# Second projection of a squared-ReLU MLP: weight loads in GpSimd's queue, residual rows summed a tile ahead, output finished in place, two early weight slots

## The chip, the core and the metric

The kernel runs on one core of one Trainium2 chip. The metric is the device time in microseconds of one execution, and what is compared is the median of several. The names of the engines are those of the profile: PE is TensorE, DVE VectorE, ACT ScalarE, POOL GpSimd, and SP SyncE, which here only issues DMA transfers.

## What is computed

One layer over 2048 rows of 1024 float32 numbers: a mixer of four head groups with its projections, then an MLP of inner width 4096 with a squared ReLU. The change concerns only the product with `w_ff2` and the sum behind it:

```python
x = x + (y @ w_out[l]).astype(x.dtype)
h = rmsnorm(x, norm_ffn[l])
x = x + (jnp.square(jax.nn.relu(h @ w_ff1[l])) @ w_ff2[l]).astype(x.dtype)
```

## The kernel before

A float32 product is made of three passes over operands that are split into a high and a low part (high by high, high by low, low by high; `PASS`). Both MLP products use one level of Strassen's method: the operands are cut into quarters, and seven products of sums of quarters replace eight. The second projection thus has seven products, in the order n = 0 to 6 (`AT` gives their numbers). Each has eight row tiles q of 128 rows by 512 columns, here written (n,q), and each tile is 16 units of the inner dimension by three passes, 48 matmuls of 128x128 by 128x512, into one PSUM bank. There are two banks, so tile (n,q+2) needs the bank of tile (n,q).

**Weights.** A unit is 128x512 of a sum of quarters of `w_ff2`. `t_unit` loads raw quarters with `raw512` into a ring of six buffers (`wr`): one for n = 0, 1, 2, three for n = 3, two for n = 4, 5, 6. DVE forms the sums by `tsub` (L1217; two for n = 3, one for n = 4, 5, 6). For n = 3 the sum is also stored to DRAM (`tt`, L1506, from GpSimd's queue), from where n = 5 loads it. `split` makes the high part on ACT (`wh`, L1207) and the low part on DVE (`wl`, L1208). The 26 slots for split units are used in turn: 9 in the ring pool (`wh`/`wl`), 15 in a pool `t2p` (`vh`/`vl`, also named wh and wl in the profile), one in buffers named `xr`, and one in `gain` (`wg`). `t2p` lies where the first projection kept its operands, so what is written there first waits until these have been stored to DRAM (`as`). Ten units of product n + 1 find a slot free while product n runs; the last six can be split only when units of n are used for the last time, in its tile q = 7. `t_unit` calls are spread over the tiles q = 3 to 7 and run at raised priority.

**Rows.** `s_tile` loads the 128 rows of a tile (the squared ReLU's Strassen operand, which the first projection stored in `as`) in two halves `sr` of 512 KB, and splits them on ACT (L1519) and DVE (L1520) into `st`, of which there are two, one tile ahead.

**Results.** A PSUM bank is emptied by ACT (n = 0, into `X`) or by sums on DVE: with `X` or into `Y`, or into the output. `finish` gives the output for n = 1, 5 and 6 (two for each tile there): it loads the residual rows `x1` into a buffer `tq` (of eight), adds `X` or `Y` to them, adds PSUM to that into a second `tq`, and stores this.

All loads and stores but those to `tt` are issued by SP, in one order for all, and a transfer that waits for its buffer holds up those behind it. A scheduler fixes the order of each engine's instructions at build time, by priority and an estimate of times; on the chip each engine goes through its list in order.

Of the kernel before, what the change touches and what calls it, by code (L numbers as in the profile page):

```python
# [16 lines left out]
ALU = mybir.AluOpType  # L17
# [4 lines left out]
P = 128  # L22
T = 2048
D = 1024
TB = 512
# [6 lines left out]
NW = 9  # L32
# [27 lines left out]
def emit(ctx, tc, a):  # L60
    nc = tc.nc
    V, S, G, PE, SY = nc.vector, nc.scalar, nc.gpsimd, nc.tensor, nc.sync
# [5 lines left out]
    x1_d = [dram.tile([TB, D], F32, name=f"x1d{b}") for b in range(NB)]  # L68
# [48 lines left out]
    c1 = p1.enter_context(tc.tile_pool(name="c1", bufs=1))  # L117
# [7 lines left out]
    def psum_mm():  # L125
        return mm.tile([P, 512], F32, tag="mm", name="mm")
# [40 lines left out]
    for r in range(2):  # L167
        G.dma_start(out=sink[r * 64:(r + 1) * 64, :],
                     in_=a["attn_sinks"].rearrange("(k r) -> r k", r=2)[r].partition_broadcast(64),
# [1028 lines left out]
    tt_d = dram.tile([NJ, P, 512], F32, name="tt")  # L1198
# [5 lines left out]
    def split(raw, pool=ring, tags=("wh", "wl"), bufs=NW):  # L1204
        h = pool.tile([P, 512], F32R, tag=tags[0], name="wh", bufs=bufs)
        l = pool.tile([P, 512], F32R, tag=tags[1], name="wl", bufs=bufs)
        S.activation(out=h, in_=raw, func=AF.Copy)  # L1207
        V.tensor_tensor(out=l, in0=raw, in1=h, op=ALU.subtract)  # L1208
        return h, l

    def raw512(src):
        r = ring.tile([P, 512], F32, tag="wr", name="wr", bufs=NR)
        SY.dma_start(out=r.rearrange("p (k c) -> p k c", k=4) if len(src.shape) == 3 else r, in_=src)
        return r

    def tsub(o, x, y, op=ALU.subtract):
        V.tensor_tensor(out=o, in0=x, in1=y, op=op)  # L1217
# [112 lines left out]
    def w2(k, half, nd):  # L1330
        return a["w_ff2"][(2 * k + half) * P:(2 * k + half + 1) * P, nd * 512:(nd + 1) * 512]


    def w_units(j, tmp, tw=None):
        f0 = j * 2 * P

        def raw(kh, fh):
            return raw512(a["w_ff1"][kh * 512:(kh + 1) * 512, f0 + fh * P:f0 + (fh + 1) * P]
                          .rearrange("(k p) c -> p k c", p=P))

        with hi_():
            a11, a12, a21, a22 = raw(0, 0), raw(1, 0), raw(0, 1), raw(1, 1)
            u = [split(a11), split(a12)]
            s1, s2 = (tw or tmpw)(), (tw or tmpw)()
            tsub(s1, a21, a22, ALU.add)
            tsub(s2, s1, a11)
            u.append(split(s2))
            u.append(split(s1))
            s3, s4 = tmp(), tmp()
            tsub(s3, a11, a21)  # L1350
            u.append(split(s3))
            tsub(s4, a12, s2)
            u.append(split(s4))
            u.append(split(a22))
        return u
# [116 lines left out]
    def tmp2():  # L1472
        return t2p.tile([P, 512], F32, tag="tq", name="tq", bufs=NT2)

    units = [0]
    NB2 = 15

    def split2(raw):
        n = units[0] % (NW + NB2 + 2)
        units[0] += 1  # L1480
        if n < NW:
            return split(raw)
        if n < NW + NB2:
            return split(raw, t2p, ("vh", "vl"), NB2)
        if n == NW + NB2:
            return split(raw, c1, ("xr", "xr"), 2)
        both = c1.tile([P, 2, 512], F32R, tag="gain", name="wg")
        S.activation(out=both[:, 0], in_=raw, func=AF.Copy)
        V.tensor_tensor(out=both[:, 1], in0=raw, in1=both[:, 0], op=ALU.subtract)
        return both[:, 0], both[:, 1]  # L1490
# [4 lines left out]
    def t_unit(n, k):  # L1495
        i = AT[n]
        with hi_():
            if i in (0, 1, 6):
                return split2(raw512(w2(k, *((0, 0), (1, 0), None, None, None, None, (1, 1))[i])))

            r = raw512(w2(k, *((1, 1), (1, 1), (1, 0), (0, 1))[i - 2]))
            x = raw512(tt_d[k] if i == 4 else w2(k, *((0, 1), (0, 1), None, (0, 0))[i - 2]))
            tsub(r, r, x)
            if i == 2:
                tsub(r, r, raw512(w2(k, 0, 0)), ALU.add)
                G.dma_start(out=tt_d[k], in_=r)  # L1506
            return split2(r)

# [2 lines left out]
    def s_tile(n, q):  # L1511
        with hi_():
            s_ = big.tile([P, 2, NJ, P], F32R, tag=("hh", "hl")[scnt[0] % 2], name="st")
            scnt[0] += 1
            for h in range(2):
                ks = slice(h * 8, h * 8 + 8)
                r = big.tile([P, 8, P], F32, tag="xt", name="sr", bufs=2)
                SY.dma_start(out=r, in_=as_d[AT[n]][q // 4][:, q % 4, ks, :])
                S.activation(out=s_[:, 0, ks], in_=r, func=AF.Copy)  # L1519
                V.tensor_tensor(out=s_[:, 1, ks], in0=r, in1=s_[:, 0, ks], op=ALU.subtract)  # L1520
        return s_

    X = t2p.tile([P, 8, 512], F32, name="X")
    Y = t2p.tile([P, 8, 512], F32, name="Y")

    def finish(q, ps, acc, tb, nd):
        b_, t0 = (q // 4) * 2 + tb, (q % 4) * P
        r = tmp2()
        SY.dma_start(out=r, in_=x1_d[b_][t0:t0 + P, nd * 512:(nd + 1) * 512])
        tsub(r, r, acc, ALU.add)  # L1530
        o = tmp2()
        tsub(o, ps, r, ALU.add)
        SY.dma_start(out=a["out"][b_ * TB + t0:b_ * TB + t0 + P, nd * 512:(nd + 1) * 512], in_=o)

    tu = {(0, k): t_unit(0, k) for k in range(NJ)}
    s_next = s_tile(0, 0)
    for n in range(7):
        for q in range(8):
            st_ = s_next
            if (n, q) != (6, 7):  # L1540
                s_next = s_tile(*((n, q + 1) if q < 7 else (n + 1, 0)))
            if n < 6 and q >= 3:
                for k in (range((q - 3) * 2, (q - 2) * 2) if q < 7 else range(8, NJ)):
                    tu[n + 1, k] = t_unit(n + 1, k)
            ps = psum_mm()
            for k in range(NJ):
                for p_, (ls, lt) in enumerate(PASS):
                    PE.matmul(ps, lhsT=st_[:, ls, k, :], rhs=tu[n, k][lt], start=k == 0 and p_ == 0,  # L1548
                              stop=k == NJ - 1 and p_ == 2)
            if n == 0:  # L1550
                S.activation(out=X[:, q], in_=ps, func=AF.Copy)
            elif n == 1:
                finish(q, ps, X[:, q], 0, 0)
            elif n == 2:
                tsub(Y[:, q], ps, X[:, q], ALU.add)
            elif n == 3:
                tsub(X[:, q], ps, X[:, q], ALU.add)
                tsub(Y[:, q], ps, Y[:, q], ALU.add)
            elif n == 4:
                tsub(X[:, q], ps, X[:, q], ALU.add)  # L1560
            elif n == 5:
                finish(q, ps, X[:, q], 1, 0)
            else:
                finish(q, ps, X[:, q], 1, 1)
                finish(q, ps, Y[:, q], 0, 1)


_INS = ["x", "w_in", "w_out", "norm_mix", "norm_ffn", "conv_w", "s5_lam_re", "s5_lam_im", "s5_b_re", "s5_b_im",
# [24 lines left out]
```

## Time and profile before

| | |
|---|---|
| time, median of 3 runs | 2293.39 us (2293.31 to 2297.61) |
| time of the profiled execution | 2296.33 us |
| its span, first to last instruction | 2294.5 us |
| mean granted TensorE clock | 0.992 of full speed |
| busy, share of the span | PE 96%, DVE 63%, ACT 42%, POOL 8% |
| first matmul of the second projection | 1647.81 us |
| its last matmul ends | 2289.24 us |

The second projection is the last 647 us of the span. The times of the rows below count from the start of the span. The profiled execution is one of its own and 2.94 us above the median. A busy share is an average over the whole; what counts in this stage is where TensorE stands still, and behind what.

### The profile page before, as it was taken

The page shows a single profiled execution, that of the slowest core. Times are in us where ns is not written, and L with a number is a line of the kernel's source. Part 1 is how long each engine was busy: PE and PEld are TensorE (multiplying, and loading weights), DVE is VectorE, ACT ScalarE, POOL GpSimd, SP SyncE. Part 2 cuts the span into 40 slices and gives each one's busy share as a digit, 9 for nine tenths or more (in the row PEclk, how much of TensorE's full clock was granted, in tenths as well). Part 3 has the DMA queues.
Part 4 walks back from the last instruction along what each step waited for, and adds up shares of the span by engine and source line. Part 5 has one row for each costly group of instructions (what it writes and reads, how often), then busy time and mean ns, then how long its engine had stood idle before and what let it go on. Part 6 is the DMA issues. An engine that isn't in the chain of part 4 may idle for free.

```text
span 2294.5 us, 32511 instructions
## 1 busy us (share of the span) xinstructions
PE 2205.3 (96%) x11460; PEld 1755.9 (77%) x11460; DVE 1449.5 (63%) x3044; ACT 961.3 (42%) x1914; POOL 194.4 (8%) x251
## 2 busy tenths in 40 slices
PE   4999999999999999999999999999999999999899
PEld 3777777777777787777788878888878877888787
DVE  4796796797679664596666676555534455465343
ACT  3444325324433433465565565555533223223121
POOL 3112212112211210000000000000000010000000
PEclk9999999999999999999999999999999999999999
DMA  6333334333443457646667575554655587475544
GB/s 174 97 89 94 98 98 138 109 105 100 139 116 104 129 195 232 196 153 202 195 196 210 151 235 156 152 148 147 201 165 195 181 293 233 146 248 175 190 165 152
DMA packets 391476, 372.97 MB, mean 163 GB/s; under 512 B 30656, under 2 KB 305184, under 8 KB 391312
## 3 DMA queue, kind: packets, MB, share of 16 engines
q1 hardware_dynamic: 388976, 365.05, 51.7%
q0 software_dynamic: 2336, 5.84, 1.0%
q8 instruction: 90, 1.47, 0.3%
q14 instruction: 74, 0.61, 0.1%
HBM read 265.97 MB, written 103.82 MB: 161 GB/s over the span
## 4 chain that ended last, share of the span: by engine, by line
PE 42%; DMA 6%; DVE 3%; ACT 1%; issue 1%; SPq 0%; DVEq 0%; ACTq 0%
PE mm L1548 19%; PE mm L1363 13%; PE hx L1363 7%; DMA wr<-in_w_ff_dram 5%; PE mx L1363 3%; DVE st L1520 1%; DMA tr<-tb 1%; DMA sr<-as 1%; DVE wr L1217 1%; DVE wl L1208 0%; ACT wh L1207 0%; ACT st L1519 0%; DMA tq<-x1d 0%; DVE tp L1217 0%; DVE tb L1327 0%
## 5 line engine op out<-in xcount | busy, mean ns | idle before, releaser
L1548 PE MATMUL mm<-wh,st 128*128 128x512 f32 x1728 | 549.2, 395 | 13.8 <-DVE tq L1217 6.1
L1548 PEld LDWEIGHTS mm<-wh,st 128*128 128x128 f32 x1728 | 325.8, 189 | 92.3 <-issue 9.6
L1548 PE MATMUL mm<-wl,st 128*128 128x512 f32 x864 | 341.1, 395 | 0.2 <-DVE wl L1208 0.2
L1363 PE MATMUL mm<-tb,wh 128*128 128x512 f32 x1024 | 323.8, 397 | 4.0 <-ACT tp L1369 1.9
L1519 ACT ACTIVATE st<-sr 128x1024 fp32r<-128x1024 f32 x112 | 115.4, 1054 | 343.6 <-PE mm L1548 244.2
L1363 PEld LDWEIGHTS mm<-tb,wh 128*128 128x128 f32 x1024 | 190.9, 189 | 53.7 <-ACT tp L1382 5.4
L510 PE MATMUL mm<-wh,hh 128*128 128x512 f32 x512 | 212.4, 415 | 0.7 <-ACT hh L505 0.7
L512 PE MATMUL mm<-wh,hl 128*128 128x512 f32 x512 | 205.9, 402 | 0.0
L105 ACT ACTIVATE wh<-wr 128x512 fp32r<-128x512 f32 x224 | 138.2, 629 | 158.6 <-PE mm L511 113.8
L511 PE MATMUL mm<-wl,hh 128*128 128x512 f32 x512 | 204.6, 400 | 0.0
L1363 PE MATMUL mm<-tb,wl 128*128 128x512 f32 x512 | 202.4, 396 | 1.0 <-DVE wl L1208 1.0
L1207 ACT ACTIVATE wh<-wr 128x512 fp32r<-128x512 f32 x204 | 124.8, 627 | 176.1 <-DVE wr L1217 83.4
L1548 PEld LDWEIGHTS mm<-wl,st 128*128 128x128 f32 x864 | 162.8, 188 | 38.9 <-DVE wl L1208 0.9
L1520 DVE TENSOR_TENSOR st<-sr,st 128x1024 fp32r<-128x1024 f32 x112 | 134.5, 1221 | 70.6 <-ACT st L1519 70.5
L111 DVE TENSOR_TENSOR wl<-wr,wh 128x512 fp32r<-128x512 f32 x224 | 150.2, 690 | 35.8 <-ACT wh L105 34.7
L1363 PE MATMUL hx<-tb,wh 128*128 128x512 f32 x512 | 161.1, 394 | 0.0
L1208 DVE TENSOR_TENSOR wl<-wr,wh 128x512 fp32r<-128x512 f32 x204 | 136.6, 687 | 36.5 <-ACT wh L1207 30.2
L510 PE MATMUL mm<-hh,wh 128*128 128x512 f32 x384 | 159.4, 415 | 0.0
L512 PE MATMUL mm<-hh,wl 128*128 128x512 f32 x384 | 152.7, 398 | 0.0
L511 PE MATMUL mm<-hl,wh 128*128 128x512 f32 x384 | 152.3, 397 | 0.0
L1363 PEld LDWEIGHTS mm<-tb,wl 128*128 128x128 f32 x512 | 96.6, 189 | 23.7 <-DVE wl L1208 1.4
L510 PEld LDWEIGHTS mm<-wh,hh 128*128 128x128 f32 x512 | 98.6, 193 | 20.8 <-ACT hh L505 1.3
(412 smaller groups left out, 3617.1 us busy)
## 6 DMA issues: line engine op xcount, KB each, us to landing
wr<-in_w_ff_dram SPq DMA_DIRECT2D x304, 256.0 KB, 3.9
as<-tp SPq DMA_DIRECT2D x224, 256.0 KB, 2.7
sr<-as SPq DMA_DIRECT2D x112, 512.0 KB, 4.6
wr<-in_w_in_dram SPq DMA_DIRECT2D x160, 256.0 KB, 3.1
wr<-in_w_out_dram SPq DMA_DIRECT2D x64, 256.0 KB, 4.0
xt<-in_x_dram SPq DMA_DIRECT2D x16, 512.0 KB, 3.6
xr<-in_x_dram SPq DMA_DIRECT2D x32, 256.0 KB, 3.0
x1d<-xr SPq DMA_DIRECT2D x32, 256.0 KB, 2.5
```

The lines of the kernel that those rows point to most:

```text
L105: S.activation(out=hi, in_=raw, func=AF.Copy)
L111: (G if le == "p" else V).tensor_tensor(out=lo, in0=raw, in1=hi, op=ALU.subtract)
L510: PE.matmul(ps, lhsT=lh, rhs=rh, start=first, stop=False)
L511: PE.matmul(ps, lhsT=lh, rhs=rl, start=False, stop=False)
L512: PE.matmul(ps, lhsT=ll, rhs=rh, start=False, stop=last)
L1207: S.activation(out=h, in_=raw, func=AF.Copy)
L1208: V.tensor_tensor(out=l, in0=raw, in1=h, op=ALU.subtract)
L1217: V.tensor_tensor(out=o, in0=x, in1=y, op=op)
L1363: PE.matmul(ps, lhsT=(wh, wl)[lw][:, ks], rhs=b[lb][:, k, :], start=first and k == 0 and q == 0, stop=k == 3 and q == 2, skip_group_check= ...
L1519: S.activation(out=s_[:, 0, ks], in_=r, func=AF.Copy)
L1520: V.tensor_tensor(out=s_[:, 1, ks], in0=r, in1=s_[:, 0, ks], op=ALU.subtract)
L1548: PE.matmul(ps, lhsT=st_[:, ls, k, :], rhs=tu[n, k][lt], start=k == 0 and p_ == 0, stop=k == NJ - 1 and p_ == 2)
```

## The change

`raw512` takes the queue as an argument, and all loads of the second projection's weights, those from `tt` too, are issued by GpSimd (`G`) instead of SP. The slots are used in another order: those named `xr` and `gain` come 10th and 11th, ahead of the 15 in `t2p`. `finish` is cut in two: `ahead` loads the residual rows and adds `X` or `Y` to them when the rows of the next tile are fetched, that is, a tile earlier; `finish` adds PSUM into the same buffer and stores it. The arithmetic stays the same.

```diff
--- before.py
+++ after.py
@@ -1208,9 +1208,9 @@
         V.tensor_tensor(out=l, in0=raw, in1=h, op=ALU.subtract)
         return h, l
 
-    def raw512(src):
+    def raw512(src, queue=SY):
         r = ring.tile([P, 512], F32, tag="wr", name="wr", bufs=NR)
-        SY.dma_start(out=r.rearrange("p (k c) -> p k c", k=4) if len(src.shape) == 3 else r, in_=src)
+        queue.dma_start(out=r.rearrange("p (k c) -> p k c", k=4) if len(src.shape) == 3 else r, in_=src)
         return r
 
     def tsub(o, x, y, op=ALU.subtract):
@@ -1480,10 +1480,10 @@
         units[0] += 1
         if n < NW:
             return split(raw)
-        if n < NW + NB2:
+        if n == NW:
+            return split(raw, c1, ("xr", "xr"), 2)
+        if n > NW + 1:
             return split(raw, t2p, ("vh", "vl"), NB2)
-        if n == NW + NB2:
-            return split(raw, c1, ("xr", "xr"), 2)
         both = c1.tile([P, 2, 512], F32R, tag="gain", name="wg")
         S.activation(out=both[:, 0], in_=raw, func=AF.Copy)
         V.tensor_tensor(out=both[:, 1], in0=raw, in1=both[:, 0], op=ALU.subtract)
@@ -1496,13 +1496,13 @@
         i = AT[n]
         with hi_():
             if i in (0, 1, 6):
-                return split2(raw512(w2(k, *((0, 0), (1, 0), None, None, None, None, (1, 1))[i])))
-
-            r = raw512(w2(k, *((1, 1), (1, 1), (1, 0), (0, 1))[i - 2]))
-            x = raw512(tt_d[k] if i == 4 else w2(k, *((0, 1), (0, 1), None, (0, 0))[i - 2]))
+                return split2(raw512(w2(k, *((0, 0), (1, 0), None, None, None, None, (1, 1))[i]), G))
+
+            r = raw512(w2(k, *((1, 1), (1, 1), (1, 0), (0, 1))[i - 2]), G)
+            x = raw512(tt_d[k] if i == 4 else w2(k, *((0, 1), (0, 1), None, (0, 0))[i - 2]), G)
             tsub(r, r, x)
             if i == 2:
-                tsub(r, r, raw512(w2(k, 0, 0)), ALU.add)
+                tsub(r, r, raw512(w2(k, 0, 0), G), ALU.add)
                 G.dma_start(out=tt_d[k], in_=r)
             return split2(r)
 
@@ -1523,22 +1523,33 @@
     X = t2p.tile([P, 8, 512], F32, name="X")
     Y = t2p.tile([P, 8, 512], F32, name="Y")
 
-    def finish(q, ps, acc, tb, nd):
-        b_, t0 = (q // 4) * 2 + tb, (q % 4) * P
-        r = tmp2()
-        SY.dma_start(out=r, in_=x1_d[b_][t0:t0 + P, nd * 512:(nd + 1) * 512])
-        tsub(r, r, acc, ALU.add)
-        o = tmp2()
-        tsub(o, ps, r, ALU.add)
-        SY.dma_start(out=a["out"][b_ * TB + t0:b_ * TB + t0 + P, nd * 512:(nd + 1) * 512], in_=o)
+
+    ENDS = {1: (("X", 0, 0),), 5: (("X", 1, 0),), 6: (("X", 1, 1), ("Y", 0, 1))}
+
+    def ahead(n, q):
+        t0, rs = (q % 4) * P, []
+        for acc, tb, nd in ENDS.get(n, ()):
+            b_ = (q // 4) * 2 + tb
+            r = tmp2()
+            SY.dma_start(out=r, in_=x1_d[b_][t0:t0 + P, nd * 512:(nd + 1) * 512])
+            tsub(r, r, (X if acc == "X" else Y)[:, q], ALU.add)
+            rs.append((r, a["out"][b_ * TB + t0:b_ * TB + t0 + P, nd * 512:(nd + 1) * 512]))
+        return rs
+
+    def finish(ps, rs):
+        for r, dst in rs:
+            tsub(r, ps, r, ALU.add)
+            SY.dma_start(out=dst, in_=r)
 
     tu = {(0, k): t_unit(0, k) for k in range(NJ)}
-    s_next = s_tile(0, 0)
+    s_next, r_next = s_tile(0, 0), []
     for n in range(7):
         for q in range(8):
             st_ = s_next
+            ends = r_next
             if (n, q) != (6, 7):
                 s_next = s_tile(*((n, q + 1) if q < 7 else (n + 1, 0)))
+                r_next = ahead(*((n, q + 1) if q < 7 else (n + 1, 0)))
             if n < 6 and q >= 3:
                 for k in (range((q - 3) * 2, (q - 2) * 2) if q < 7 else range(8, NJ)):
                     tu[n + 1, k] = t_unit(n + 1, k)
@@ -1549,8 +1560,6 @@
                               stop=k == NJ - 1 and p_ == 2)
             if n == 0:
                 S.activation(out=X[:, q], in_=ps, func=AF.Copy)
-            elif n == 1:
-                finish(q, ps, X[:, q], 0, 0)
             elif n == 2:
                 tsub(Y[:, q], ps, X[:, q], ALU.add)
             elif n == 3:
@@ -1558,11 +1567,7 @@
                 tsub(Y[:, q], ps, Y[:, q], ALU.add)
             elif n == 4:
                 tsub(X[:, q], ps, X[:, q], ALU.add)
-            elif n == 5:
-                finish(q, ps, X[:, q], 1, 0)
-            else:
-                finish(q, ps, X[:, q], 1, 1)
-                finish(q, ps, Y[:, q], 0, 1)
+            finish(ps, ends)
 
 
 _INS = ["x", "w_in", "w_out", "norm_mix", "norm_ffn", "conv_w", "s5_lam_re", "s5_lam_im", "s5_b_re", "s5_b_im",
```

The order of instructions changes with it. On DVE, around the end of tile (2,3): `wr<-wr,wr` are the sums of weights for n = 3, `st` the low parts of rows, and the last line is the sum that empties the bank of (2,3). Before:

```order
L1520 TENSOR_TENSOR st_18083<-sr_18084,st_18083 128x1024
L1217 TENSOR_TENSOR wr_18457<-wr_18457,wr_18462 128x512
L1217 TENSOR_TENSOR wr_18470<-wr_18470,wr_18472 128x512
L1520 TENSOR_TENSOR st_18083<-sr_18088,st_18083 128x1024
L1217 TENSOR_TENSOR wr_18470<-wr_18470,wr_18475 128x512
L1217 TENSOR_TENSOR wr_18483<-wr_18483,wr_18485 128x512
L1217 TENSOR_TENSOR wr_18483<-wr_18483,wr_18488 128x512
L1217 TENSOR_TENSOR Y_16625<-mm_18118,X_16624 128x512
```

Of the change:

```order
L1520 TENSOR_TENSOR st_18074<-sr_18075,st_18074 128x1024
L1217 TENSOR_TENSOR wr_18475<-wr_18475,wr_18477 128x512
L1520 TENSOR_TENSOR st_18074<-sr_18079,st_18074 128x1024
L1217 TENSOR_TENSOR wr_18475<-wr_18475,wr_18480 128x512
L1217 TENSOR_TENSOR wr_18488<-wr_18488,wr_18490 128x512
L1217 TENSOR_TENSOR wr_18488<-wr_18488,wr_18493 128x512
L1217 TENSOR_TENSOR wr_18501<-wr_18501,wr_18503 128x512
L1217 TENSOR_TENSOR Y_16625<-mm_18109,X_16624 128x512
```

Each piece has five sums, but those of the change belong to later units: counted from the first of n = 3, the bank's sum stands behind 29 sums and stood behind 26. For (2,2) it is 24 and was 20, for the second use of the bank of (3,0) 43 and was 40.

In POOL's list at n = 3, the change (`wr<-in_w_ff2` are the loads):

```order
L1506 DMA tt_10115<-wr_18338 128x512
L1213 DMA wr_18425<-in_w_ff2_dram 128x512
L1213 DMA wr_18428<-in_w_ff2_dram 128x512
L1213 DMA wr_18436<-in_w_ff2_dram 128x512
L1213 DMA wr_18438<-in_w_ff2_dram 128x512
L1506 DMA tt_10115<-wr_18351 128x512
L1213 DMA wr_18441<-in_w_ff2_dram 128x512
L1213 DMA wr_18449<-in_w_ff2_dram 128x512
L1506 DMA tt_10115<-wr_18423 128x512
```

Before, POOL had only the stores to `tt` there, and the loads were SP's; these are the last of them:

```order
L1506 DMA tt_10115<-wr_18457 128x512
L1506 DMA tt_10115<-wr_18470 128x512
L1506 DMA tt_10115<-wr_18483 128x512
L1506 DMA tt_10115<-wr_18496 128x512
L1506 DMA tt_10115<-wr_18509 128x512
L1506 DMA tt_10115<-wr_18522 128x512
```

The stores now stand in one order with the loads of later units.

On DVE at tile (5,1), before; the last two lines add `X` to the residual rows and PSUM to that:

```order
L1520 TENSOR_TENSOR st_19952<-sr_19953,st_19952 128x1024
L1217 TENSOR_TENSOR wr_20397<-wr_20397,wr_20399 128x512
L1520 TENSOR_TENSOR st_19952<-sr_19957,st_19952 128x1024
L1217 TENSOR_TENSOR wr_20406<-wr_20406,wr_20408 128x512
L1217 TENSOR_TENSOR tq_19946<-tq_19946,X_16624 128x512
L1217 TENSOR_TENSOR tq_19949<-mm_19897,tq_19946 128x512
```

Of the change, where the last line is the sum with PSUM of (5,1):

```order
L1520 TENSOR_TENSOR st_19881<-sr_19886,st_19881 128x1024
L1217 TENSOR_TENSOR wr_20373<-wr_20373,wr_20375 128x512
L1217 TENSOR_TENSOR tq_20340<-tq_20340,X_16624 128x512
L1217 TENSOR_TENSOR wr_20382<-wr_20382,wr_20384 128x512
L1217 TENSOR_TENSOR wr_20391<-wr_20391,wr_20393 128x512
L1217 TENSOR_TENSOR tq_19827<-mm_19893,tq_19827 128x512
```

The residual sum of (5,1) stands further ahead, out of this piece, and the `tq` sum here is that for a later tile; the last sum of weights in front of the finishing sum, the 79th from the first of n = 3, has moved behind it.

## Rows read from the trace of the kernel before

**Rows 1.** Stretches: us, busy (xcount) by engine, PEclk, DMA share, GB/s.

```profile
1822.00:1910.00 88.00, 84.66 (x359) 66.61 (x358) 50.67 (x68) 22.09 (x28) 8.22 (x15) 1.00 0.80 272
1910.00:1997.00 87.00, 85.87 (x373) 69.75 (x372) 48.91 (x64) 25.88 (x32) 0.54 (x1) 1.00 0.64 205
1997.00:2085.00 88.00, 88.00 (x381) 71.19 (x380) 46.18 (x59) 25.73 (x32) 0.00 (x0) 1.00 0.59 187
2085.00:2172.00 87.00, 80.92 (x340) 65.23 (x339) 44.80 (x58) 23.75 (x30) 0.00 (x0) 0.96 0.66 213
```

**Rows 2.** TensorE's waits, 1647 to 2294.5: total us, times, longest.

```profile
PE mm L1548 <- DVE tq L1217: 6.1, 1, 6.1
PE mm L1548 <- DVE st L1520: 2.4, 3, 1.3
PE mm L1548 <- ACT wh L1207: 2.3, 1, 2.3
PE mm L1548 <- DVE Y L1217: 1.8, 2, 1.1
PE mm L1548 <- ACT X L1551: 1.0, 1, 1.0
```

**Rows 3.** DVE in order of time: start us, us, what [idle before <-releaser].

```profile
1826.82 0.69 DVE L1217 TENSOR_TENSOR wr<-wr 128x512 f32<-128x512 f32 x1 [0.47 <-DMA wr<-in_w_ff_dram]
...
1886.99 0.68 DVE L1217 TENSOR_TENSOR Y<-mm,X 128x512 f32<-128x512 f32 x1
...
1888.54 1.22 DVE L1520 TENSOR_TENSOR st<-sr,st 128x1024 fp32r<-128x1024 f32 x1
...
1895.81 0.69 DVE L1217 TENSOR_TENSOR wr<-wr 128x512 f32<-128x512 f32 x1 [3.38 <-DMA tt<-wr]
```

**Rows 4.** TensorE in order of time, tile (2,5).

```profile
1887.82 0.47 PE L1548 MATMUL mm<-wh,st 128*128 128x512 f32 x1 [0.64 <-DVE Y L1217]
...
1889.82 0.74 PE L1548 MATMUL mm<-wh,st 128*128 128x512 f32 x2 [1.31 <-DVE st L1520]
```

**Rows 5.** DVE groups, 1822 to 1910: busy us, mean ns, idle before, releasers.

```profile
L1217 DVE TENSOR_TENSOR wr<-wr 128x512 f32<-128x512 f32 x30 | 20.6, 690 | 32.1 <-DMA wr<-in_w_ff_dram 28.6 <-DMA tt<-wr 3.4
```

**Rows 6.** DMA issues, 1822 to 1910: count, KB, median us to landing.

```profile
wr<-in_w_ff_dram SPq DMA_DIRECT2D x45, 256.0 KB, 4.7
...
tt<-wr POOLq DMA_DIRECT2D x15, 256.0 KB, 4.6
```

**Rows 7.** POOL's groups, 1822 to 1910; its DMA issues before 1647.

```profile
L1506 POOL DMA_DIRECT2D tt<-wr x15 | 8.2, 548 | 697.4 <-DVE wr L1217 697.4
...
wgr<-in_s_w_glu_dram POOLq DMA_DIRECT2D x2, 256.0 KB, 4.4
```

**Rows 8.** Waits of SP's queue, 1822 to 1910.

```profile
SPq L1518 <- DVE st L1520: 12.8, 11, 2.6
```

**Rows 9.** DVE in order of time, tile (3,1).

```profile
1950.94 0.69 DVE L1217 TENSOR_TENSOR wr<-wr 128x512 f32<-128x512 f32 x1 [0.39 <-DMA wr<-in_w_ff_dram]
```

**Rows 10.** TensorE in order of time, tile (3,2).

```profile
1947.32 0.48 PE L1548 MATMUL mm<-wh,st 128*128 128x512 f32 x1 [1.13 <-DVE Y L1217]
```

**Rows 11.** DVE in order of time, tile (5,2).

```profile
2133.50 0.69 DVE L1217 TENSOR_TENSOR wr<-wr 128x512 f32<-128x512 f32 x1 [1.19 <-DMA wr<-in_w_ff_dram]
...
2140.96 0.69 DVE L1217 TENSOR_TENSOR tq<-tq,X 128x512 f32<-128x512 f32 x1 [1.81 <-DMA tq<-x1d]
2141.68 0.69 DVE L1217 TENSOR_TENSOR tq<-mm,tq 128x512 f32<-128x512 f32 x1
```

**Rows 12.** TensorE in order of time, tile (5,3).

```profile
2142.52 0.77 PE L1548 MATMUL mm<-wh,st 128*128 128x512 f32 x1 [6.08 <-DVE tq L1217]
...
2147.35 0.86 PE L1548 MATMUL mm<-wh,st 128*128 128x512 f32 x2
```

**Rows 13.** The chain that ended last, 1655 to 1676.

```profile
1658.64 0.71 SPq L1529
...
1659.45 7.00 DMA wr<-in_w_ff_dram
```

## The prediction

> **What bounds the kernel now.** The busy times by stretch come first. In the second projection TensorE works 84 to 88 us of every 88 [rows 1]; an undisturbed stretch is full, 88.0 us for 383 matmuls, so 48 matmuls, one tile, take 11.03 us. The change leaves the 2688 matmuls of this stage as they are and can only win or lose the holes between them. The list of TensorE's waits says what the holes are [rows 2]: one of 6.1 us on a `tq` sum, three of together 2.4 us on `st`, one of 2.3 us on `wh`, two of together 1.8 us on `Y`, one of 1.0 us on `X`, 13.6 us in all. The granted clock adds to it: after the 6.1 us hole the matmuls from 2142.52 to about 2147.85 take twice as long [rows 12], half clock (1.2 instead of 2.4 GHz), so 2.7 us of those 5.3 are lost. With this, some 16.3 us stand to be won, and no more except at the end of the kernel.
>
> Next, what DVE does ahead of each hole, by the timeline. A PSUM bank is free for the next tile but one only when DVE has done its `Y`, `X` or `tq` sum, and DVE works in order. In front of `Y` at 1886.99 stand sums that wait for weight loads; TensorE starts tile (2,5) right behind it, at 1887.82, and then waits 1.31 us more for `st`, which stands behind `Y` too [rows 3, 4]. So in the tiles of n=2 the pace of the 32 sums of the next product decides. Of their 30 in this stretch DVE waits 32.1 us [rows 5], mostly for loads.
>
> That pace is set by a ring of six buffers: a unit of n=3 takes three, and its `r` buffer comes free when the store to `tt` has landed. Two units later the buffer is loaded again: 4.7 us for a load, 4.6 for a store [rows 6], 0.69 for each of one or two sums [rows 5], so some 10.3 us for two units. The trace has 28 sums, 14 units, from 1826.82 to 1895.81 [rows 3], 9.9 us for two. The agreement says that the ring, not SP's queue, is what limits here.
>
> **The change, part by part.**
>
> *Early slots and the free queue, n=0.* TensorE waits 2.3 us for `wh` and 1.0 for `X` in tile (0,1) [rows 2]. The chain there leads back to a weight load that SP issued only at 1659.45, right behind an `x1` load, and that took 7.00 us [rows 13]. In POOL's queue only weights stand ahead of it, and two more units have slots that need no `as` store to land. TensorE came to the missing unit 2.3 us before it got it; issued at the same time, a load of POOL's 4.4 us [rows 7] would be 2.6 us earlier. I take −3.0; bounds −3.3 and 0 (if the last units still wait for the stores).
>
> *Residual sums a tile ahead, n=5.* The 6.1 us hole is DVE waiting for an `x1` load at 2140.96, then the `tq` sum at 2141.68 [rows 11, 12]. The load is on its way long before in the new order, and the residual sum of (5,1) is done. What is left ahead of the finishing sum is the sum that ran at 2133.50 and no longer the one after it: 2133.50 + 0.69 + 0.69 = 2134.9, while TensorE wants the bank at 2142.52 − 6.08 = 2136.44. That hole goes, with its half clock: −8.8. If the weight sums are slower on the other queue some of it returns; I take 1.0, so −7.8, bounds −8.8 and −4.
>
> *Finishing in place.* After the last matmul there are two sums in place of three: −0.7 by a sum's 690 ns [rows 5]. The number of DVE instructions is unchanged otherwise.
>
> *Loads from POOL's queue.* All weight and `tt` loads of the stage move from SP to POOL. What a load costs there: the two loads of this size that POOL issued earlier landed in 4.4 us, SP's in this stretch in 4.7 [rows 6, 7]; POOL's 15 stores take 548 ns to issue [rows 7]. Lower bound of what a ring cycle gets longer by: 0; upper: the issue of a load and a store, 1.1 us in 9.9. On SP the loads also stood behind `sr` loads that waited 12.8 us for `st` [rows 8]; that goes. The gain and the cost are of one size; I let the 29th sum come 2 us earlier, bounds 7 us either way (a tenth of the 69 us from the first sum).
>
> *The order on DVE.* This is what the queue change does besides, and what I think decides. More sums stand ahead of the bank releases: ahead of `Y` of (2,2) 24 instead of 20, of (2,3) 29 instead of 26, ahead of the second release of (3,0) 43 instead of 40 (counted from the first sum of n=3). By the times of before the 29th sum starts at 1895.81 [rows 3]; 0.6 later comes `Y`, then `st` for 1.22, so that TensorE would do the second unit of (2,5) at about 1898.4. Without holes it would be there at 1889.82 − 1.31 − 0.64 − the 1.1 of the two other `st` waits [rows 2, 4] = 1886.8, less about 0.5 for smaller gaps: 1886.3. The stretch would lose 12.1 where it now loses 3.3 [rows 1]: +8.8; with the sums 2 us earlier +6.8. Bounds: +1.8 and +15.8 by the 7 us above.
>
> The same for n=3: the 43rd sum ran at 1950.94 [rows 9]; `Y` then ends 1952.2. TensorE wanted the bank at 1947.32 − 1.13 = 1946.2 [rows 10], and the hole would be 6.1 where the stretch loses 1.1 [rows 1]: +5.0. Bounds: 0 (the sums come sooner) and +8.2 (each of the three added sums waits the 1.07 us that a sum waits on average [rows 5]).
>
> *Clock.* A hole of 6 us was followed by half clock that cost 2.7 [rows 12]; in the stretch with the holes of about 1 us it stayed at 1.00 [rows 1]. The hole of (3,1) to (3,2) would be of the first kind: +2.7, and for those of n=2, of some 4 us each, I add 0.7. Bounds 0 and 8 (three such).
>
> *A rule against this.* POOL's 15 stores were issued while DVE was busy 50.67 of 88 us, mostly with two-input sums, and took 548 ns on average [rows 1, 7], so none was held up. The Trainium skill, "GPSIMD Engine Reference", Specifications, says that POOL shares its SBUF interfaces with DVE and contends with DVE instructions of two SBUF inputs; "SBUF — State Buffer", SBUF: two separate sides, adds that a DMA issued by GpSimd is starved of descriptors while DVE runs in a two-port mode. By that rule a load could wait out a DVE instruction; the trace doesn't show it yet, so it stays a rival below.
>
> **Sum.** −3.0 −7.8 −0.7 +6.8 +5.0 +3.4 = +3.7 us. The profiled execution took 2296.33 us, 1.83 more than its span and 2.94 more than the median, and the difference goes onto the median: 2293.4 + 3.7 = 2297.1 us.
>
> **Rivals.**
>
> *The sums come sooner (faster).* If POOL's own queue shortens a ring cycle by a tenth, the 29th sum is 7 us earlier (+1.8), the 43rd some 2.5 (+2.5), no hole is long enough for the clock: −3.0 −8.8 −0.7 +1.8 +2.5 = −8.2, so 2285.2 us. For it: SP's 12.8 us behind `st` [rows 8]. Against: the ring explains the pace without SP. It decides from 4 us earlier on. Beyond it, all holes gone: −16.3 −0.7, 2276.4 us.
>
> *POOL is the slower queue (slower).* Stores now stand in order behind loads that wait for earlier stores. At a tenth per cycle: n=2 +15.8, n=3 +7.5, n=5 −5, clock +5, and −3.7 for the rest: +19.6; at a twentieth about +11. So 2304 to 2313 us. Against it: 4.4 us to landing [rows 7].
>
> *DVE holds POOL up (slower).* If each issue waited for a DVE instruction of 0.69 us, a cycle with its load and store would be 1.4 us longer in 9.9, and the sum +22 to +25: 2317 us. Against it: 548 ns.
>
> *The early slots don't help:* the last units of n=0 wait for the `as` stores as before, and the `wh` hole stays: 3 us more, inside the range of the first case.
>
> **How the numbers follow.** Chances: the forecast with its own range of 2289 to 2302 us 0.45; sums sooner 0.25; all holes gone 0.07; POOL slower 0.16; held up 0.07. A measurement of this kernel can tell about 0.2%, 4.6 us, from no change. Of the forecast's 0.45 I give 0.30 to within and 0.15 to above 2298; so faster 0.32, same 0.30, slower 0.38. The range leaves out the two outermost cases and a little: 2279 to 2310 us.
>
> **What would show it.** Right: no wait of TensorE on `tq` left, waits on `Y` grown to over 15 us in n=2 and n=3, in front of each of them a DVE sum that waits for a load; a half clock after the longest. Wrong: if the 29th sum of n=3 comes over 4 us sooner after the first than 69 us, or if POOL's issues grow well beyond 0.55 us.

## The result, and the profile after

The changed kernel takes 2307.91 us (median of 5 runs, 2306.22 to 2317.49), the one before 2294.89 us (5 runs, 2293.31 to 2297.61): a ratio of 1.0064, 95% interval 1.0041 to 1.0086. It is slower by 13 us. The profiled execution of the change is its slowest, 2317.49 us with a span of 2315.7; its second projection begins 4.7 us later (1652.5 instead of 1647.8). Little that runs before that was changed, and the nine variants below that leave the number of raw buffers alone began it between 1642.6 and 1648.1; I count these 4.7 us as this execution's own, without having shown it.

From the first matmul of each product to the first of the next (the last column to the end of the last matmul), in us, from the times of the matmuls in the two traces:

| | n=0 | 1 | 2 | 3 | 4 | 5 | 6 | all |
|---|---|---|---|---|---|---|---|---|
| before | 93.0 | 88.7 | 94.4 | 89.7 | 89.4 | 97.7 | 88.6 | 641.4 |
| change | 93.3 | 89.1 | 106.7 | 97.2 | 90.4 | 93.0 | 88.9 | 658.6 |

A product without holes takes some 88.5. Of the 17.2 us lost, n = 2 has 12.3 and n = 3 7.5; n = 5 gives 4.7 back. TensorE's waits in the stage, to be read against [rows 2] (total, times, longest):

```profile
PE mm L1559 <- DVE Y L1217: 16.0, 4, 6.4
PE mm L1559 <- ACT X L1562: 3.3, 1, 3.3
PE mm L1559 <- DVE tq L1217: 1.9, 1, 1.9
PE mm L1559 <- DVE st L1520: 1.5, 4, 0.4
PE mm L1559 <- ACT wh L1207: 0.6, 1, 0.6
```

What was one hole of 6.1 us on `tq` is now 16.0 us on `Y` in four. The stretches of n = 2 and n = 3, to [rows 1] (the last three columns are granted clock, DMA share and GB/s):

```profile
1822.00:1910.00 88.00, 77.26 (x307) 59.78 (x306) 48.40 (x65) 21.38 (x28) 32.09 (x60) 0.93 0.76 254
1910.00:2000.00 90.00, 83.57 (x351) 67.57 (x350) 46.68 (x60) 25.64 (x32) 18.83 (x36) 0.96 0.60 197
```

TensorE's clock, 1.00 before in both, was granted at 0.93 and 0.96. DVE at the first and the 29th sum of n = 3, then `Y` of (2,3) and `st`, and TensorE behind it:

```profile
1835.01 0.69 DVE L1217 TENSOR_TENSOR wr<-wr 128x512 f32<-128x512 f32 x1 [3.96 <-DMA wr<-in_w_ff_dram]
...
1904.29 0.69 DVE L1217 TENSOR_TENSOR wr<-wr 128x512 f32<-128x512 f32 x1 [4.02 <-DMA wr<-in_w_ff_dram]
1904.90 0.68 DVE L1217 TENSOR_TENSOR Y<-mm,X 128x512 f32<-128x512 f32 x1
1905.50 2.35 DVE L1520 TENSOR_TENSOR st<-sr,st 128x1024 fp32r<-128x1024 f32 x2
```

```profile
1905.73 0.77 PE L1559 MATMUL mm<-wh,st 128*128 128x512 f32 x1 [5.46 <-DVE Y L1217]
1906.30 0.63 PE L1559 MATMUL mm<-wl,st 128*128 128x512 f32 x1
```

28 sums took 69.28 us; before it was 68.99 [rows 3]. The pace is the same, but `Y` stands behind the 29th sum, which waits 4.02 us for a load, and not the 26th. The start is not the same: the first sum waits 3.96 us for its load (0.47 before) and runs 0.1 us after the first matmul of n = 2, where before it ran 2.8 us ahead of it. Counted from that matmul the 29th sum comes after 69.4 us in place of 66.2. TensorE stands 5.46 us, and its next matmuls take 0.63 where one took 0.39 or 0.40: half clock. The same at (3,1) to (3,2), where the second release stands behind the 43rd sum [rows 9, 10]:

```profile
1968.83 0.68 DVE L1217 TENSOR_TENSOR wr<-wr 128x512 f32<-128x512 f32 x1
1969.43 0.68 DVE L1217 TENSOR_TENSOR Y<-mm,Y 128x512 f32<-128x512 f32 x1
```

```profile
1970.25 0.77 PE L1559 MATMUL mm<-wh,st 128*128 128x512 f32 x1 [6.43 <-DVE Y L1217]
```

The loads themselves: time to landing, and POOL's issues, in the stretch of [rows 6, 7]:

```profile
wr<-in_w_ff_dram POOLq DMA_DIRECT2D x46, 256.0 KB, 4.7
...
tt<-wr POOLq DMA_DIRECT2D x14, 256.0 KB, 4.7
```

```profile
L1213 POOL DMA_DIRECT2D wr<-in_w_ff_dram x46 | 24.6, 537 | 122.3 <-DVE wl L1208 75.3 <-DVE wr L1217 33.4 <-DMA tt<-wr 5.1
```

4.7 us to landing is what SP's loads took there; an issue takes 537 ns, beside DVE that was busy 48.40 of 88 us.

At n = 5 a smaller hole is left, 1.9 us on `tq`. DVE ahead of it, to [rows 11]:

```profile
2160.68 0.69 DVE L1217 TENSOR_TENSOR tq<-tq,X 128x512 f32<-128x512 f32 x1 [1.42 <-DMA tq<-x1d]
2161.29 0.68 DVE L1217 TENSOR_TENSOR wr<-wr 128x512 f32<-128x512 f32 x1
2163.09 0.69 DVE L1217 TENSOR_TENSOR wr<-wr 128x512 f32<-128x512 f32 x1 [1.11 <-DMA wr<-in_w_ff_dram]
2163.70 0.68 DVE L1217 TENSOR_TENSOR tq<-mm,tq 128x512 f32<-128x512 f32 x1
```

The `tq<-tq,X` at 2160.68 is a residual sum of tile (6,0), made ahead, and it waits 1.42 us for its own `x1` load, whose buffer an output store had only just left; two sums and the release of (5,1) queue behind it. The edit brought a wait of the kind that it removed; whether this wait makes the hole, a run below tells.

### The profile page after: what moved, and what is told of

Read it like the earlier page. It is cut to its first block, busy times and chain, and to the rows that moved or that the text cites. A ratio compares the mean times of both kernels' runs of the same rounds, so it can differ in the third digit from the quotient of the medians.

```text
span 2315.7 us, 32567 instructions
## 1 busy us (share of the span) xinstructions
PE 2216.7 (96%) x11460; PEld 1763.3 (76%) x11460; DVE 1448.3 (63%) x3044; ACT 961.5 (42%) x1914; POOL 295.8 (13%) x443
## 5 line engine op out<-in xcount | busy, mean ns | idle before, releaser
L1559 PE MATMUL mm<-wh,st 128*128 128x512 f32 x1728 | 555.3, 399 | 23.4 <-DVE Y L1217 16.0
L1207 ACT ACTIVATE wh<-wr 128x512 fp32r<-128x512 f32 x204 | 125.2, 627 | 191.7 <-DVE wr L1217 97.7
L1213 POOL DMA_DIRECT2D wr<-in_w_ff_dram x176 | 94.5, 538 | 846.2 <-DMA as<-tp 402.7
```

The costliest lines, as they stand in the source:

```text
L1213: queue.dma_start(out=r.rearrange("p (k c) -> p k c", k=4) if len(src.shape) == 3 else r, in_=src)
```

## The experiments

Theory 1 is that of the prediction: with the loads in a queue of their own the scheduler, which estimates that they land early, puts more weight sums ahead of the sums that empty PSUM; on the chip the weight sums come no sooner, and DVE's order holds TensorE up. Theory 2: POOL is the slower queue, so the weights come late. Ratios are to the kernel before in the same session, with 95% intervals.

**Undo the queue.** One line in `raw512`:

```diff
     def raw512(src, queue=SY):
+        queue = SY
```

> The change without the move of the loads: weights are issued by SP again, the two early slots, the residual sums a tile ahead and the finishing in place stay. On DVE the bank releases then stand behind as many weight sums as before (8, 14, 20, 26 for n = 2). Theory 1 (the order on DVE costs the time) and theory 2 (POOL is the slower queue) both expect the holes of n = 2 and n = 3 to go back to about 6 us together and the 6 us hole of n = 5 to stay away: some 9 us less than before, 2284 to 2288 us. A third theory, that the other edits cost time as well, expects no less than before.

2288.59 us, ratio 0.9964 (0.9951 to 0.9978). Products: 92.6, 89.1, 95.2, 89.1, 89.6, 88.6, 88.9. TensorE's waits:

```profile
PE mm L1560 <- DVE Y L1218: 3.3, 3, 1.7
PE mm L1560 <- ACT X L1563: 2.6, 1, 2.6
PE mm L1560 <- DVE st L1521: 0.7, 2, 0.3
```

No wait on `tq` is left, and n = 5 takes 88.6 in place of 97.7: the edits besides the queue are worth what was forecast for n = 5. The queue costs about 1%.

**The queue alone.** The kernel before, with `G` for its 192 loads of `w_ff2` and `tt`.

> The kernel before with nothing changed but the queue of the weight loads (POOL). On DVE the releases stand behind 11, 17, 24, 29 sums as in the change. Theories 1 and 2 both expect holes in n = 2 and n = 3 as in the change, some 25 us with the half clock behind them, against 6.5 before; the hole at n = 5 shrinks since no weight load stands ahead of the x1 loads on SP, but not to nothing: 2303 to 2312 us.

2309.98 us, 1.0065 (1.0046 to 1.0085): products 92.3, 88.7, 106.5, 97.7, 90.8, 95.8, 88.6, holes as in the change. These two runs place the loss in the queue, but don't tell the theories apart. The next two do, in the main.

**Weights on POOL, in the old order.** The loads of rows go to POOL's queue as well, so that weights queue behind them as they did on SP, and the scheduler sees it:

```diff
-                SY.dma_start(out=r, in_=as_d[AT[n]][q // 4][:, q % 4, ks, :])
+                G.dma_start(out=r, in_=as_d[AT[n]][q // 4][:, q % 4, ks, :])
```

> The change, with the loads of the rows (sr) put into POOL's queue too, so that weights wait behind rows as they did on SP. On DVE the releases then stand behind 8, 13, 18, 22 sums, fewer than even before, while every weight load is still POOL's. Theory 1 expects the holes of n = 2 and n = 3 to be small again: 2284 to 2291 us. Theory 2 expects them to stay, since the loads are no faster: 2305 us or more.

**Weights on SP, in the new order.** The same line, with the loads of weights back on SP.

> The reverse: weights on SP, the rows (sr) on POOL. On DVE the releases stand behind 11, 18, 26, 30 sums, a little more than in the change, while all weight loads come from SP. Theory 1 expects holes in n = 2 and n = 3 as in the change or larger: 2306 us or more. Theory 2 expects them gone: 2288 us or less.

| weights issued by | releases of (2,1), (2,2), (2,3) behind | ratio | n=2 | n=3 | 28 sums |
|---|---|---|---|---|---|
| SP (queue undone) | 14, 20, 26 sums | 0.9964 | 95.2 | 89.1 | 70.6 us |
| POOL, rows on POOL too | 13, 18, 22 | 0.9995 (0.9981 to 1.0008) | 94.0 | 98.2 | 75.2 |
| POOL (the change) | 17, 24, 29 | 1.0064 | 106.7 | 97.2 | 69.3 |
| SP, rows on POOL | 18, 26, 30 | 1.0063 (1.0041 to 1.0085) | 106.0 | 99.3 | 69.3 |

With the new order, or one a sum or two beyond it, n = 2 takes 106 us, whichever queue issues the weights; with an order like the old one it takes 94 to 95 (in three more runs below with SP's order, 95.6 to 97.5). So theory 2 falls as the main cause for n = 2, but a part of it can be left. The last row has its releases further back than the change and its sums sooner: counted from the first matmul of n = 2 the 29th comes after 66.8 us, in the change after 69.4. Some 2 to 3 us of the 12 may thus be late loads on POOL; the change's own order with the weights on SP was not run. In this table the new order also goes with rows and weights in separate queues; the separation by itself does not slow the sums, 69.3 us for 28 in both rows.

At n = 5 it is theory 2 that fits. The release of (5,1) stands behind 78 sums in the last row as in the change, and a residual sum just ahead of it waits for `x1` too, 1.35 us:

```profile
2153.34 0.69 DVE L1218 TENSOR_TENSOR tq<-tq,X 128x512 f32<-128x512 f32 x1 [1.35 <-DMA tq<-x1d]
2153.97 0.69 DVE L1218 TENSOR_TENSOR wr<-wr 128x512 f32<-128x512 f32 x1
2154.58 0.68 DVE L1218 TENSOR_TENSOR tq<-mm,tq 128x512 f32<-128x512 f32 x1
```

Yet no wait of TensorE on `tq` is left there, and n = 5 takes 89.2 us against 93.0. The 78th sum comes 31.7 us after the first matmul of n = 5, in the change 33.9; there it waits 1.11 us for a weight load that POOL issued at 2159.56, while DVE was still waiting for `x1`. So the residual sum did not hold that load up. The two runs differ in the rows' queue as well, and why the loads on POOL are late there is not shown.

The run of 2295.1 us with all on POOL is 4 us above its expectation, and why shows in its waits (the run with weights on SP below it):

```profile
PE mm L1559 <- DVE Y L1217: 7.3, 1, 7.3
PE mm L1559 <- DVE st L1520: 2.8, 2, 2.5
```

```profile
PE mm L1560 <- DVE Y L1218: 15.9, 4, 8.0
PE mm L1560 <- DVE st L1521: 2.9, 5, 0.9
```

Its one hole of 7.3 us on `Y` is at n = 3, where the release stands behind 40 sums as before, so the order isn't the cause of that one; the sums are late there, 75.2 us for 28 and 28.1 from the 33rd to the 43rd (24.7 before, 26.3 in the change), which would fit weights and rows that wait for each other in one queue; that was not tried apart. So POOL's queue can cost something when all goes through it. In the change as it was made the order costs more at n = 2.

**One release moved.** The change, loads on POOL, with the PSUM sums of n = 2 and 3 at raised priority (`with hi_():` around the two branches). Of the counts at holes only that of the second release of (3,0) moves, 43 to 39.

> The change itself, loads on POOL, with the sums that empty PSUM in n = 2 and n = 3 raised to the priority of the weight units. Of the places that hold TensorE only one moves much: the second release of (3,0) stands behind 39 weight sums instead of 43; n = 2 keeps 17, 24, 29. Theory 1 (the order): the hole at (3,1) to (3,2), 6.6 us and 2.4 of half clock behind it, falls under 2 us in all, those of n = 2 stay; 2299 to 2303 us, ratio to before 1.002 to 1.004 instead of 1.0064. Theory 2 (POOL is slow, whatever the order): the hole stays, as the 39th sum or its weights are late as well: ratio 1.006.

2302.89 us, 1.0037 (1.0016 to 1.0058): products 91.8, 89.1, 106.4, 92.4, 89.6, 92.7, 88.9. n = 3 gets 4.8 us back by one instruction's place, n = 2 stays. The hole doesn't go altogether: 1.8 us and the half clock behind it come back one tile later, where the release still stands behind 45 sums. Its waits on `Y`, 16.0 in the change:

```profile
PE mm L1559 <- DVE Y L1217: 11.7, 4, 4.7
```

**A larger ring.** Nine raw buffers in place of six, on SP and on POOL; three of them in `t2p`, for three of the residual buffers:

```diff
-NT2 = 8
+NT2 = 5
...
-        r = ring.tile([P, 512], F32, tag="wr", name="wr", bufs=NR)
+        pool, tag, bufs = ring, "wr", NR
+        if units2[0] is not None:
+            units2[0] += 1
+            if units2[0] % 9 < 3:
+                pool, tag, bufs = t2p, "wq", 3
+        r = pool.tile([P, 512], F32, tag=tag, name="wr", bufs=bufs)
```

> The kernel with the loads back on SP, and with nine raw weight buffers instead of six (three more in the pool t2p, paid with three of the eight residual buffers). Theory: the ring of six and its way over tt set the pace of the sums; the 28 sums from the 1st to the 29th of n = 3, 70.6 us there, then take a third less, some 47 to 52 us, and the holes of n = 2 (about 6 us) go, though the releases of n = 2 stand behind more sums (12, 20, 25, 31): 2280 to 2285 us. Rival: the transfers themselves (their engines 80% busy there) set the pace; the 28 sums stay above 62 us and the holes grow as in the change: 2300 us or more.

> The change, loads on POOL, with the same nine raw weight buffers (five residual buffers). The releases of n = 2 stand behind 14, 22, 28, 32 sums. Theory (ring): 28 sums in some 47 to 54 us instead of 69.3, most of the holes of n = 2 go, the one of n = 3 too: 2283 to 2292 us. Rival (the transfers set the pace): 2305 us or more.

Both were wrong: 2319.86 us (1.0104, 1.0071 to 1.0137) and 2341.33 us (1.0192, 1.0159 to 1.0225). The first three sums now run 70 us ahead of the rest, so the span from the first to the 29th (134.8 us) says nothing; from the 4th to the 29th it is 55.6 us on SP, where six buffers took 63.9, and 60.7 on POOL, where six took 65.2. So the ring does hold the pace, but half as much again of it gives 13% and 7%, not a third. The transfers took a little longer, 5.1 us for loads and 5.7 for stores on SP, in place of 4.9 and 5.4 with six buffers there; that is too little to explain the rest, which stays open:

```profile
wr<-in_w_ff_dram SPq DMA_DIRECT2D x46, 256.0 KB, 5.1
...
tt<-wr POOLq DMA_DIRECT2D x15, 256.0 KB, 5.7
```

And on SP n = 2 took 95.0 us, no less than with six: more sums stand ahead again (the releases stand behind 20, 25, 31). What made these kernels slow lies elsewhere (TensorE's waits, on SP):

```profile
PE mm L1568 <- ACT wh L1207: 14.6, 1, 14.6
PE mm L1568 <- ACT st L1527: 11.6, 2, 6.9
```

14.6 us of wait for the first weights, ahead of the stage, and 11.6 on rows that ACT splits late. The extra buffers lie in `t2p`, whose first writes wait for the `as` stores, which would explain the first; that was not tried apart. On POOL the longest wait is another, 17.0 us on `Y` at (4,1), whose release stands behind 63 sums in place of 54 in the change.

**The early slots.** On SP, with `xr` and `gain` put back behind the 15 slots of `t2p` (the lines of `split2` as before).

> The kernel with the loads back on SP, and with the two early slots put back to the end of the 26: the residual sums a tile ahead and the finishing in place are all that is left of the change. If the early slots gain what I forecast, this is some 3 us slower than with them (ratio to before about 0.9975 instead of 0.9964). If the hole of tile (0,1), which stayed at 4.7 us with the half clock behind it, is not touched by them, it is the same within 1.5 us.

2287.11 us, 0.9971 (0.9956 to 0.9986), the same as with them (0.9964). n = 0 takes 92.4 instead of 92.6. The early slots bring nothing measurable; 1 or 2 us these intervals could not tell.

**ACT's copy first.** On SP:

```diff
             if n == 0:
-                S.activation(out=X[:, q], in_=ps, func=AF.Copy)
+                with hi_():
+                    S.activation(out=X[:, q], in_=ps, func=AF.Copy)
```

> The kernel with the loads back on SP, and with ACT's copies of PSUM into X (n = 0) raised in priority; that of tile (0,0) then stands eight instructions further ahead on ACT, in front of weight splits that wait for loads. If the hole of (0,1) is an order of ACT, its 2.6 us and the 1.7 of half clock behind it shrink to under 1.5: some 3 us less than without, ratio to before about 0.995. If it is the late weights themselves, the wait moves to wh and nothing is gained.

2285.70 us, 0.9952 (0.9932 to 0.9971). n = 0 falls from 92.6 to 88.2: the hole at the end of (0,1) and its half clock are gone, 4.4 us. It was an order too, on another engine: in the change's trace ACT (here at the end of the hole) does the copy right behind a split that waited for its load, with others ahead of it:

```profile
1676.82 0.63 ACT L1207 ACTIVATE wh<-wr 128x512 fp32r<-128x512 f32 x1 [0.70 <-DMA wr<-in_w_ff_dram]
1677.36 1.07 ACT L1562 ACTIVATE X<-mm 128x512 f32<-128x512 f32 x2
```

**Towards a faster version.** On top of that, on SP, the releases at raised priority, and in another run the units of n = 1 and up at none (`hi_()` left away in `t_unit`):

> The fastest so far (loads on SP, ACT's copies into X raised) with the same raised priority of the releases; only n = 3 moves, (3,0) from 40 sums to 38. Its hole there is 1.7 us: at most 2 us less, ratio to before 0.994 to 0.9955.

> The fastest so far with the units of the next products (n of 1 and up) at no raised priority: the releases of n = 2 stand behind 8, 13, 19, 26, 29 sums instead of 8, 14, 20, 26, 30, that of (3,0) behind 37. Theory 1 expects the hole of (2,4) to (2,5) to shrink a little and that of n = 3 to go: 1 to 4 us less, ratio 0.9935 to 0.995; if the weights themselves come too late then, waits on wh at n = 3 and a ratio above 0.996.

2281.27 us, 0.9939 (0.9920 to 0.9959), and 2281.38 us, 0.9926 (0.9898 to 0.9954). In the second the products take 88.2, 89.1, 90.7, 88.3, 89.6, 88.6, 88.9, and this is all that TensorE waits for in the stage:

```profile
PE mm L1561 <- DVE Y L1218: 0.6, 1, 0.6
PE mm L1561 <- DVE st L1522: 0.3, 1, 0.3
```

Its releases of n = 2 stand behind 8, 13, 19, 26 and 29 sums. It keeps the residual sums ahead, the finishing in place and the slots, and beats both kernels; its sums of n = 4 are slower than before (30.4 us from the 33rd to the 43rd, against 24.7), which costs nothing since nobody waits behind them.

## Why the prediction came out as it did

The time lies inside the range, the direction was the likeliest of the three, and the mechanism that I gave as deciding, the order on DVE, is the one that the runs show at n = 3 and, for the greater part, at n = 2. The size was not right: the forecast of 2297.1 us was 11 us short, and 2307.91 lies outside its own 2289 to 2302, in the 2304 to 2313 of the rival in which POOL is the slower queue. That rival's working, a ring cycle a tenth longer, does not show in n = 2, where 28 sums took as long as before; loads that come late on POOL do, at n = 5. That the range held is thus in part luck. Of the signs, the waits on `Y` (16.0 us in all), the half clock and the 537 ns came as stated, and "no wait of TensorE on `tq` left" did not (1.9 us). Step by step, by the two traces:

- *n = 2, +6.8 and 0.7 for the clock.* Measured 12.3. The step that failed is "I let the 29th sum come 2 us earlier": measured from the first matmul of n = 2 it came 3.1 us later, 0.3 by the pace and 2.8 because the first sum itself was late, a start that I had taken over from before. The clock term was too small as well: tile (2,5), behind the last hole, took 13.6 us where others take 11.1, so some 2.4 where I had given 0.7. The two misses make 6.8 us. The whole is off by 4.8 because n = 2 before had lost 5.7 us against n = 1 (94.4 and 88.7), and not only the 3.3 of idle time that I subtracted.
- *n = 3, +5.0 and 2.7.* Measured 7.5 in place of 7.7; the hole was 6.43, forecast 6.1.
- *Early slots and the free queue, −3.0.* Measured +0.3: the wait for `wh`, 2.3 us, is gone there (the 0.6 us of the list is at (4,1)), but that for `X` grew from 1.0 to 3.3, with half clock behind it (tile (0,2) 12.7 us, before 11.2). I had followed the chain to the late load and had not asked what else stood behind it on ACT. The hole needed the copy's place, not the slots.
- *n = 5, −7.8.* Measured −4.7. The 1.0 that I kept back for slower sums was 4.1: 1.9 us of hole and the half clock behind it. With the weights on SP this product had no hole, with the same 78 sums ahead of the release too, so what I had put too low is the lateness of POOL's loads here. The 1.42 us that the residual sum waits is not shown to add to it.
- *n = 4, nothing.* Measured +1.0, with the second release of (3,7) behind two more sums; it ends 0.15 us before TensorE goes on at (4,1).
- *Tail, −0.7.* From the last matmul's end to the span's end 5.3 before and 4.6 after.
- *Rivals.* Sums sooner: no, they kept their pace. POOL slower: at n = 5 yes, and when rows went through it too; at n = 2 not in the pace, for 2 to 3 us perhaps in the start. POOL held up by DVE: 537 ns for each issue, as the stores before (548). So the rule of the Trainium skill ("GPSIMD Engine Reference", Specifications) that DVE instructions with two SBUF inputs contend with POOL does not show in these 46 issues. What DVE's two-port modes would do, no run here shows.

The 17.2 us of the stage less 0.7 at the tail are more than the 13 us between the medians: the profiled execution of the change is 9.6 us above its median, that of before 1.4.

What stays open: why this execution's stage began 4.7 us late, why the first sum of n = 3 and the sums ahead of (5,1) came late with the weights on POOL, and how much of the pace of n = 3 is the ring and how much the transfers.

## What to carry to other kernels

Moving transfers to a queue of their own changes more than who issues them: here the scheduler put what uses them further ahead on an in-order engine (that it believes the loads earlier is read from that order, not shown). Ask, for each instruction that TensorE waits for, behind how many load-bound ones it stands before and after, and read from the trace when those really ran; here four places in a list were worth 5 us. If the pace of the loads is set by buffers, a freer queue can't raise it, and the instructions that free PSUM belong ahead of the work for the next product.

## What the runs showed of the hardware

Loads of 256 KB landed in 4.7 us from either queue; POOL took 537 ns for an issue, with DVE's two-input sums running beside it. Holes of TensorE of 3.2 us and more in the change were followed by matmuls at half clock, and so was one of 1.9 us, while the holes of 0.64 and 1.31 us before [rows 4] were not. The length of the hole alone does not decide it: the one of 2.26 us on `wh` before was followed by full clock, two matmuls in 0.63 us.

```profile
1667.15 0.50 PE L1548 MATMUL mm<-wh,st 128*128 128x512 f32 x1 [2.26 <-ACT wh L1207]
...
1668.68 0.63 PE L1548 MATMUL mm<-wh,st 128*128 128x512 f32 x2
```

Half as many raw buffers again shortened the pace of the sums by 13% with the loads on SP and by 7% with them on POOL.
